# Evacuating filler banks with priority, and transposing the GLA keys ahead of the values, in a hybrid decoder layer

## The chip, the cores and the metric

The kernel runs on one core of a Trainium2 chip. Times are device microseconds of one execution, from which a median over several runs is taken. The profile is of one execution. In it PE is TensorE's matmul queue, PEld its weight loads (they overlap with PE), DVE is VectorE, ACT is ScalarE, POOL is GpSimd, and SP issues most of the DMAs. L548 is line 548 of the kernel before.

## What is computed

One decoder layer on 512 tokens of width 1024, in float32:

- RMS norm of x, and one projection `w_in` that gives everything the two mixers need.
- A sparse attention (NSA) with 8 query heads in two key/value groups: compressed blocks, selected blocks (all 8 of 8 here), and a window of 256, each with its own softmax and a gate.
- A chunked gated linear attention (GLA) with 4 heads of key width 64 and value width 128, in chunks of 64: a state per chunk, decayed and added up from chunk to chunk, and an output from the chunk itself and from the state before it, then a norm and a gate.
- The two branches are projected, gated by a sigmoid (the merge) and summed, projected by `w_out` and added to x.
- A cross attention to 256 memory tokens, and a gated feed-forward layer of width 2816 with a convolution of width 3; each behind an RMS norm and added to x. A final RMS norm.

```
h = rms_norm(x, ln_mix_g)
q_a, kv_a, gate_a, q_b, k_b, v_b, r_b, alpha_b, merge = split(h @ w_in)
mix = sigmoid(merge_1) * (nsa(...) @ w_branch_nsa) + sigmoid(merge_2) * (gla(...) @ w_branch_gla)
x = x + mix @ w_out
x = x + memory_cross_attention(rms_norm(x), mem_n, ...)
x = x + conv_ffn(rms_norm(x), ...)
return rms_norm(x, ln_final_g)
```

## The kernel before

**Products.** Activations lie transposed, width on the partitions and the 512 tokens along the free axis. Each float32 operand is split in a high half (rounded to fp32r) and a low half (the rest), and each product is three matmuls: high by high, high by low, low by high (`mm3`, L159 to L162). `split` (L164 to L166) makes the halves: ACT copies into the high half (L165), DVE subtracts to get the low one (L166). `scaled_split` (L201 to L203) does it with a factor.

**Weights.** They come as 141 blocks of 128 x 1024 in the order of use. `take` (L153) hands out a block and makes `convert` (L130) prepare two blocks further: SP loads it (L126), ACT makes the high half (L140), and an engine out of the list `lo_engine`, by the block's number, makes the low half (L141). For the last eight blocks this is done in halves of 512 columns (L148 and L149). The list holds DVE alone at first; after the first four blocks it is DVE and GpSimd in turn, until the products that compress keys and values are done (L471), and DVE alone from then on.

**Banks.** PSUM has eight banks in four tags: `acc` 2, `sc` 3, `pt` 2, `o` 1. A tile of a tag waits until one of the tag's banks has been read for the last time. SBUF tiles come in tags too: `t` has 6 tiles of 512 columns, `s` 16, and `g` 43.

**Order.** Instructions are written in program order, and a scheduler orders them on each engine ahead of time, by its own estimate of when each is ready, with program order as the priority. Each engine then works through its queue in that order. What a block of code issued under high priority, its instructions go ahead of others that are ready at the same time.

**Fillers.** The attention stage (`nsa_scores`, `nsa_values`) is full of softmax work for DVE and ACT. Between its steps `fill` (L506) issues closures out of a list, each a dense product of 24 matmuls (`dense8`) into an `acc` bank, which is then evacuated: `gla_r` (four; its bank is read by DVE at L548, then ACT and GpSimd go on), `gla_q` (two, L523) and `gla_k` (two, L533). In the GLA stage the fillers are eight `nsa_part`: for each even one two merge products come first (`merge`, bank read by DVE at L717, then a tanh on ACT at L718), and each has a branch product (`branch`) whose bank is read at L741.

**GLA stage.** In program order: what is left of the fillers, the value projection (`dense_tok` into four banks, then `scaled_split` of each), and then for each of two pairs of heads (m): `gla_qk` splits queries and keys (L796 to L801), `gla_keys` transposes the decayed keys by four matmuls into a bank of tag `pt` (L750) and splits them into two `t` tiles, `gla_att` makes the scores within the chunks (L809) and masks them (L813), `gla_states` makes the increments (L764) into three banks of tag `sc` and one of `pt`, chains them on DVE (L774, L776) and splits the states, and `gla_out` (L834 to L844) and `gla_norm` (L243, L227, L228, L855, L856) finish a head. One `fill` stands between most of these steps:

```
    qk = {(0, a): gla_qk(0, a) for a in range(2)}
    ks = gla_keys(0)
    a0 = gla_att(*qk[0, 0])
    st = gla_states(0, *ks)
    fill(GLA_FILL[0])
    ...
    gla_norm(*o)
    o = gla_out(0, 1, st[1], *a1)
    ks = gla_keys(1)
    fill(GLA_FILL[3])
```

**The end.** The second half of the down projection makes the first 384 tokens of each of eight output tiles (`head_mm`, L160 to L162). `head_out` adds the residual (L1128) and calls `add_square`: ACT squares (L214), and GpSimd adds to the running sum (L224). After the first four tiles two tiny activations (L1137, L1138) bring in the table with the square root ahead of its use. The other 128 tokens follow, and among their matmuls the norm of the first 384 (`norm_head`, `scale_head`).

Of the kernel before, what the change touches and what calls it, by code (L numbers as in the profile page):

```python
# [16 lines left out]
P = 128  # L17
# [41 lines left out]
def layer_kernel(ctx: ExitStack, tc: tile.TileContext, xT, memT, W, small, const, gfin, out, out_t, order):  # L59
# [319 lines left out]

    V2 = [None] * 4  # L380
    pb = [bank(t) for t in ("sc", "sc", "pt", "o")]
    for b0, nk in ((0, 3), (3, 3), (6, 2)):
        w = take(("BB", b0, nk))
        for j in range(nk):
            k = b0 + j
            c = slice(j * BW, (j + 1) * BW)
            for t in range(4):
                ts = slice(t * P, (t + 1) * P)
                o = pb[t][:, :BW]
                nc.tensor.matmul(o, xg[k][0][:, ts], w[0][:, c], start=k == 0, stop=False)  # L390
                nc.tensor.matmul(o, xg[k][0][:, ts], w[1][:, c], start=False, stop=False)
                nc.tensor.matmul(o, xg[k][1][:, ts], w[0][:, c], start=False, stop=k == KT - 1)
    xk = cmp_inputs(pkc, S("pos_k"))
# [77 lines left out]
    lo_engine[:] = [nc.vector]  # L471
# [42 lines left out]
    def gla_q(m):  # L514
        def go():
# [7 lines left out]
            nc.vector.scalar_tensor_tensor(q, ps, 0.125, rstd, op0=ALU.mult, op1=ALU.mult)  # L523
# [4 lines left out]
    def gla_k(m):  # L528
        def go():
# [3 lines left out]
            nc.vector.tensor_mul(kf, ps, rstd)  # L533
# [10 lines left out]
    def gla_r(hd):  # L544
        def go():
            ps = dense8(("A", "w_in", C_RB + hd * P), xg)
            rf, th = t_(), t_()
            nc.vector.tensor_mul(rf, ps, rstd)  # L548
# [156 lines left out]
    fill(99)  # L705
    pb = [bank(t) for t in ("acc", "acc", "sc", "sc")]
# [7 lines left out]
    def merge(col, m, tile_):  # L714
        ps = dense8(("A", "w_in", col + m * P), xg)
        th = tile_()
        nc.vector.tensor_mul(th, ps, rstd)  # L717
        nc.scalar.activation(th, th, AF.Tanh, scale=0.5)  # L718
        return th
# [15 lines left out]
    def nsa_part(n):  # L735
        def go():
# [4 lines left out]
            nc.vector.scalar_tensor_tensor(pm[n], pm[n], 1.0, ps, op0=ALU.add, op1=ALU.mult)  # L741
# [4 lines left out]

    def gla_keys(m):
        pk = bank("pt")
        for t in range(4):
            nc.tensor.transpose(pk[:, t * P:(t + 1) * P], ksd[m][:, t * P:(t + 1) * P], C("ident"))  # L750
        kh, kl = t_(F32R), t_(F32R)
        split(kh, kl, pk)
        return kh, kl
# [108 lines left out]
    ks = gla_keys(0)  # L862
# [6 lines left out]
    o = gla_out(0, 0, st[0], *a0)  # L869
    fill(GLA_FILL[2])  # L870
    gla_norm(*o)
    o = gla_out(0, 1, st[1], *a1)
    ks = gla_keys(1)
# [253 lines left out]
    def head_out(ps, n):  # L1127
        nc.vector.tensor_add(x2[n][:, head], ps, x2[n][:, head])  # L1128
        add_square(sqs, x2[n][:, head], CUT)
# [7 lines left out]
    nc.scalar.activation(warm, x2[0][:, 0:1], AF.Square)  # L1137
    nc.scalar.activation(warm, warm, AF.Sqrt)  # L1138
    for n in range(4, 8):
# [3 lines left out]
        head_out(ps, n)  # L1143
    gt = sb([P, 1024], F32, "raw", 3)
# [171 lines left out]
```

## Time and profile before

| | us |
|---|---|
| median of 3 runs | 865.82 (863.78 to 866.4) |
| the profiled execution | 864.57 |
| its span, first to last instruction | 862.7 |
| PE busy | 847.2 |
| DVE busy | 565.8 |
| ACT busy | 425.0 |
| POOL busy | 176.6 |

The granted clock of TensorE was 0.998 of full speed over the span. Busy times count an engine's own instructions; matmuls are pipelined, and their ends are modelled, so a matmul's row is longer than the distance to the next one. An idle time in square brackets stands before the instruction, with what ended it.

### The profile page before, as it was taken

To read this page: it belongs to the slowest core of one execution; us is meant where nothing else is said; L and a number is where in the kernel's file an instruction comes from. 1 tells how busy PE (TensorE), PEld (TensorE's weight loads), DVE (VectorE), ACT (ScalarE), POOL (GpSimd) and SP (SyncE) were. 2 spreads that over 40 slices of the span, in tenths; PEclk is the share of its full clock that TensorE was granted. 3 is DMA by queue.
4 is the path that set the end of the run, shared out by engine and by line. 5 is a ranking of instruction groups with operands and counts; after the bars stand their busy time and mean duration, and the time that the engine had idled before them with its cause. 6 is when DMAs were issued, how large, how long until landed. Compare 5 with 4: busy or idle time off the path is not lost.

```text
span 862.7 us, 11076 instructions
## 1 busy us (share of the span) xinstructions
PE 847.2 (98%) x4172; PEld 706.4 (82%) x4172; DVE 565.8 (66%) x923; ACT 425.0 (49%) x742; POOL 176.6 (20%) x157
## 2 busy tenths in 40 slices
PE   9999999999999999999999999999999999999997
PEld 6988788777877888898888888888888888888996
DVE  7576898989979677454587759665533465565324
ACT  8466878787444455344455545433311333334311
POOL 2373354412000023203200412111000111112121
PEclk9999999999999999999999999999999999999999
DMA  8332210102221242254331132222222222222302
GB/s 292 115 131 98 74 50 25 49 25 74 74 91 57 74 147 98 97 178 147 123 115 49 65 110 96 98 98 97 98 98 98 97 98 98 97 98 98 123 25 98
DMA packets 26406, 83.58 MB, mean 97 GB/s; under 512 B 3056, under 2 KB 5104, under 8 KB 26352
## 3 DMA queue, kind: packets, MB, share of 16 engines
q1 hardware_dynamic: 26064, 82.58, 27.5%
q8 instruction: 33, 0.54, 0.2%
q10 hardware_dynamic: 288, 0.28, 0.1%
q14 instruction: 21, 0.17, 0.1%
HBM read 80.76 MB, written 2.10 MB: 96 GB/s over the span
## 4 chain that ended last, share of the span: by engine, by line
PE 87%; DVE 5%; ACT 4%; issue 1%; POOL 1%; DMA 0%; DVEq 0%; ACTq 0%; POOLq 0%
PE up_ps_sc L162 4%; PE up_ps_sc L161 4%; PE up_ps_sc L160 4%; PE fill_ps_acc L160 3%; PE fill_ps_acc L161 3%; PE fill_ps_acc L162 3%; PE up_ps_pt L162 3%; PE up_ps_pt L161 3%; PE up_ps_pt L160 3%; PE up_ps_acc L162 3%; PE up_ps_acc L161 3%; PE up_ps_acc L160 3%; PE nsa_ps_o L663 2%; PE nsa_ps_pt L669 2%; PE down_ps_sc L162 2%; PE down_ps_sc L161 2%
## 5 line engine op out<-in xcount | busy, mean ns | idle before, releaser
L1086 POOL TENSOR_TENSOR up_s<-up_s,up_s 128x512 f32<-128x512 f32 x22 | 35.8, 1630 | 259.1 <-ACT up_wh L140 207.0
L141 DVE TENSOR_TENSOR up_wl<-up_raw,up_wh 128x1024 fp32r<-128x1024 f32 x40 | 63.0, 1575 | 15.4 <-ACT up_wh L140 15.3
L140 ACT ACTIVATE up_wh<-up_raw 128x1024 fp32r<-128x1024 f32 x40 | 42.5, 1061 | 60.9 <-PE up_ps_sc L161 31.9
L160 PE MATMUL up_ps_sc<-xo_g,up_wh 128*128 128x512 f32 x124 | 48.3, 390 | 0.0
L162 PE MATMUL up_ps_sc<-xo_g,up_wl 128*128 128x512 f32 x124 | 48.3, 389 | 0.0
L161 PE MATMUL up_ps_sc<-xo_g,up_wh 128*128 128x512 f32 x124 | 48.3, 389 | 0.0
L160 PE MATMUL up_ps_pt<-xo_g,up_wh 128*128 128x512 f32 x104 | 40.5, 389 | 0.0
L162 PE MATMUL up_ps_pt<-xo_g,up_wl 128*128 128x512 f32 x104 | 40.5, 389 | 0.0
L161 PE MATMUL up_ps_pt<-xo_g,up_wh 128*128 128x512 f32 x104 | 40.5, 389 | 0.0
L160 PE MATMUL fill_ps_acc<-in_g,fill_wh 128*128 128x512 f32 x96 | 38.4, 400 | 0.8 <-DVE fill_t L548 0.8
L161 PE MATMUL fill_ps_acc<-in_g,fill_wh 128*128 128x512 f32 x96 | 38.1, 397 | 0.0
L162 PE MATMUL fill_ps_acc<-in_g,fill_wl 128*128 128x512 f32 x96 | 37.9, 395 | 0.0
L631 ACT ACTIVATE nsa_s<-nsa_s,nsa_nm 128x128 f32<-128x128 f32 (+3 forms) x64 | 34.2, 538 | 6.5 <-DVE nsa_nm L622 6.5
L160 PE MATMUL up_ps_acc<-xo_g,up_wh 128*128 128x512 f32 x88 | 34.3, 389 | 0.0
L162 PE MATMUL up_ps_acc<-xo_g,up_wl 128*128 128x512 f32 x88 | 34.3, 389 | 0.0
L161 PE MATMUL up_ps_acc<-xo_g,up_wh 128*128 128x512 f32 x88 | 34.2, 389 | 0.0
L1082 ACT ACTIVATE up_s<-up_s 128x512 f32<-128x512 f32 x22 | 13.8, 632 | 40.4 <-DVE up_s L1080 40.4
L140 ACT ACTIVATE down_wh<-down_raw 128x1024 fp32r<-128x1024 f32 x9 | 9.5, 1061 | 39.4 <-PE down_ps_sc L161 17.5
L165 ACT ACTIVATE nsa_pth<-nsa_ps_pt 128x512 fp32r<-128x512 f32 x38 | 21.9, 593 | 11.0 <-PE nsa_ps_pt L669 10.7
L161 PEld LDWEIGHTS up_ps_sc<-xo_g,up_wh 128*128 128x128 f32 x124 | 23.3, 188 | 4.9
L160 PEld LDWEIGHTS up_ps_sc<-xo_g,up_wh 128*128 128x128 f32 x124 | 23.3, 188 | 4.8
L162 PEld LDWEIGHTS up_ps_sc<-xo_g,up_wl 128*128 128x128 f32 x124 | 23.3, 188 | 4.8
(975 smaller groups left out, 2687.6 us busy)
## 6 DMA issues: line engine op xcount, KB each, us to landing
up_raw<-in_w SPq DMA_DIRECT2D x44, 512.0 KB, 3.2
fill_raw<-in_w SPq DMA_DIRECT2D x20, 512.0 KB, 3.2
down_raw<-in_w SPq DMA_DIRECT2D x18, 512.0 KB, 3.2
proj_raw<-in_w SPq DMA_DIRECT2D x14, 512.0 KB, 3.8
mix_raw<-in_w SPq DMA_DIRECT2D x12, 512.0 KB, 3.2
mkv_raw<-in_w SPq DMA_DIRECT2D x8, 512.0 KB, 3.3
wout_raw<-in_w SPq DMA_DIRECT2D x8, 512.0 KB, 3.4
in_s<-in_xT SPq DMA_DIRECT2D x8, 256.0 KB, 5.4
```

Of the source, the lines that this page charges most:

```text
L140: nc.scalar.activation(wh[:, c], r[:, c], AF.Copy)
L141: lo.tensor_tensor(wl[:, c], r[:, c], wh[:, c].bitcast(F32), op=ALU.subtract)
L160: nc.tensor.matmul(ps, w[0], x[0], start=first, stop=False)
L161: nc.tensor.matmul(ps, w[0], x[1], start=False, stop=False)
L162: nc.tensor.matmul(ps, w[1], x[0], start=False, stop=last)
L165: nc.scalar.activation(h, src, AF.Copy)
L631: nc.scalar.activation(s[:, :w], s[:, :w], AF.Exp, scale=sl, bias=nm[:, c:c + 1], accum_out=sums[:, c:c + 1])
L663: nc.tensor.matmul(po, v, x, start=j == 0 and x is parts[0], stop=j == last and x is parts[-1])
L669: nc.tensor.transpose(pt[:, g * P:(g + 1) * P], srcs[g], C("ident"))
L1082: nc.scalar.activation(cv, cv, AF.Gelu_apprx_tanh)
L1086: nc.gpsimd.tensor_tensor(gm, gm, cv, op=ALU.mult)
```

## The change

- A helper `evacuate` issues one operation at high priority. Five operations that read a filler's bank go through it: in `gla_q`, `gla_k`, `gla_r`, `merge` (also used in the mix stage) and `nsa_part`.
- `gla_keys` is defined earlier, and the keys of the first pair are transposed and split before the value projection. Those of the second pair come right after the first head's output, ahead of one more filler and of the second head's output. Their halves lie in `g` tiles instead of `t` tiles.
- `lo_engine` becomes DVE alone earlier: right after the blocks of the values, gates and alphas.
- In `head_out` the sums of squares are added on DVE instead of GpSimd.
- The two tiny activations for the square root's table come after the sixth tile instead of after the fourth.

```
+    def evacuate(op, *args, **kw):
+        with tc.high_priority():
+            op(*args, **kw)
...
+    lo_engine[:] = [nc.vector]
     xk = cmp_inputs(pkc, S("pos_k"))
...
     cmp_hidden("cmp_w1_v", xv, hid[0:62, P:2 * P], 1)
-    lo_engine[:] = [nc.vector]
...
-            nc.vector.scalar_tensor_tensor(q, ps, 0.125, rstd, op0=ALU.mult, op1=ALU.mult)
+            evacuate(nc.vector.scalar_tensor_tensor, q, ps, 0.125, rstd, op0=ALU.mult, op1=ALU.mult)
...
-            nc.vector.tensor_mul(kf, ps, rstd)
+            evacuate(nc.vector.tensor_mul, kf, ps, rstd)
...
-            nc.vector.tensor_mul(rf, ps, rstd)
+            evacuate(nc.vector.tensor_mul, rf, ps, rstd)
...
     stage[0] = "gla"
     fill(99)
+
+    def gla_keys(m):
+        pk = bank("pt")
+        for t in range(4):
+            nc.tensor.transpose(pk[:, t * P:(t + 1) * P], ksd[m][:, t * P:(t + 1) * P], C("ident"))
+        kh, kl = g_(F32R), g_(F32R)
+        split(kh, kl, pk)
+        return kh, kl
+
+    ks = gla_keys(0)
     pb = [bank(t) for t in ("acc", "acc", "sc", "sc")]
     dense_tok("w_in", C_VB, xg, pb)
...
-        nc.vector.tensor_mul(th, ps, rstd)
+        evacuate(nc.vector.tensor_mul, th, ps, rstd)
...
-            nc.vector.scalar_tensor_tensor(pm[n], pm[n], 1.0, ps, op0=ALU.add, op1=ALU.mult)
+            evacuate(nc.vector.scalar_tensor_tensor, pm[n], pm[n], 1.0, ps, op0=ALU.add, op1=ALU.mult)
...
-    def gla_keys(m):
-        pk = bank("pt")
-        for t in range(4):
-            nc.tensor.transpose(pk[:, t * P:(t + 1) * P], ksd[m][:, t * P:(t + 1) * P], C("ident"))
-        kh, kl = t_(F32R), t_(F32R)
-        split(kh, kl, pk)
-        return kh, kl
...
     qk = {(0, a): gla_qk(0, a) for a in range(2)}
-    ks = gla_keys(0)
     a0 = gla_att(*qk[0, 0])
...
     o = gla_out(0, 0, st[0], *a0)
+    ks = gla_keys(1)
     fill(GLA_FILL[2])
     gla_norm(*o)
     o = gla_out(0, 1, st[1], *a1)
-    ks = gla_keys(1)
     fill(GLA_FILL[3])
...
-        add_square(sqs, x2[n][:, head], CUT)
+        add_square(sqs, x2[n][:, head], CUT, eng=nc.vector)
...
     for n in range(4):
         head_out(banks[n], n)
-    nc.scalar.activation(warm, x2[0][:, 0:1], AF.Square)
-    nc.scalar.activation(warm, warm, AF.Sqrt)
     for n in range(4, 8):
...
         head_out(ps, n)
+        if n == 5:
+            nc.scalar.activation(warm, x2[n][:, 0:1], AF.Square)
+            nc.scalar.activation(warm, warm, AF.Sqrt)
```

## Rows read from the trace of the kernel before

**Rows 1.** The page's first part: busy time, share of the span and instruction count of each engine.

```profile
PE 847.2 (98%) x4172; PEld 706.4 (82%) x4172; DVE 565.8 (66%) x923; ACT 425.0 (49%) x742; POOL 176.6 (20%) x157
```

**Rows 2.** The view of waits, for the matmul queue alone: the waiting group, what released it, the total in us, how often, the longest.

```profile
PE fill_ps_acc L160 <- DVE fill_g L717: 1.5, 1, 1.5
...
PE gla_ps_sc L764 <- ACT gla_t L165: 1.2, 2, 0.8
PE nsa_ps_o L663 <- DVE nsa_ptl L166: 1.1, 2, 0.6
PE down_ps_sc L162 <- DVE down_g L149: 0.8, 2, 0.5
PE fill_ps_acc L160 <- DVE fill_t L548: 0.8, 1, 0.8
PE proj_ps_acc L162 <- POOL proj_wl L141: 0.5, 1, 0.5
PE nsa_ps_pt L669 <- DVE nsa_s L639: 0.4, 2, 0.2
PE gla_ps_sc L764 <- DVE gla_t L813: 0.3, 1, 0.3
PE gla_ps_sc L764 <- DVE gla_s L203: 0.2, 1, 0.2
```

**Rows 3.** The view of stretches: from and to in us, length, then the busy time (and instruction count) of PE, of its weight loads, of DVE, ACT and POOL, the granted clock, the DMA share and GB/s.

```profile
42.00:52.00 10.00, 9.48 (x64) 7.94 (x63) 7.57 (x20) 8.22 (x13) 5.23 (x7) 1.00 0.29 102
...
60.00:75.00 15.00, 15.00 (x108) 12.59 (x107) 9.04 (x15) 8.60 (x13) 7.89 (x6) 1.00 0.58 199
...
100.00:140.00 40.00, 38.48 (x201) 31.52 (x200) 35.84 (x117) 31.35 (x82) 16.20 (x18) 1.00 0.15 51
...
210.00:217.00 7.00, 6.14 (x43) 4.83 (x42) 6.22 (x13) 4.52 (x9) 0.00 (x0) 1.00 0.00 0
250.00:275.00 25.00, 22.66 (x124) 18.31 (x124) 24.26 (x39) 12.21 (x20) 1.05 (x2) 1.00 0.11 38
...
312.00:810.00 498.00, 497.88 (x2301) 416.53 (x2300) 295.91 (x352) 201.91 (x287) 78.98 (x50) 1.00 0.31 107
```

**Rows 4.** The timeline of DVE around 118 us, in the sparse attention: start, length, engine, line, operation, output and inputs, shapes, count, and the idle time before it with its releaser.

```profile
118.15 0.85 DVE L688 TENSOR_TENSOR nsa_t<-nsa_ps_o,nsa_t 64x256 f32<-64x256 f32 x2 [1.33 <-ACT nsa_t L683]
119.03 0.69 DVE L548 TENSOR_TENSOR fill_t<-fill_ps_acc,proj_rstd 128x512 f32<-128x512 f32 x1
```

**Rows 5.** The same view around 271 us, in the GLA stage. PE first, then DVE.

```profile
269.91 0.39 PE L161 MATMUL fill_ps_acc<-in_g,fill_wh 128*128 128x512 f32 x1
270.14 0.39 PE L162 MATMUL fill_ps_acc<-in_g,fill_wl 128*128 128x512 f32 x1
...
265.72 3.00 DVE L776 SCALAR_TENSOR_TENSOR gla_s<-gla_s,fill_dec,gla_ps_sc 64x128 f32<-64x128 f32 x8
...
272.64 0.69 DVE L717 TENSOR_TENSOR fill_g<-fill_ps_acc,proj_rstd 128x512 f32<-128x512 f32 x1
```

**Rows 6.** The same view around 256 us, where the second pair's key transposes are split. PE first, then ACT.

```profile
256.77 0.50 PE L764 MATMUL gla_ps_sc<-gla_s,gla_t 64*128 64x256 f32 x4 [0.84 <-ACT gla_t L165]
...
256.14 0.57 ACT L165 ACTIVATE gla_t<-gla_ps_pt 128x512 fp32r<-128x512 f32 x1
```

**Rows 7.** The same view from 211 to 215.5 us, at the end of the value projection. PE first, then DVE.

```profile
212.86 0.38 PE L764 MATMUL gla_ps_sc<-gla_s,gla_t 64*128 64x256 f32 x1 [0.38 <-ACT gla_t L165]
...
215.17 0.39 PE L764 MATMUL gla_ps_sc<-gla_s,gla_t 64*128 64x256 f32 x1 [0.29 <-DVE gla_t L813]
...
213.29 0.68 DVE L166 TENSOR_TENSOR gla_t<-gla_ps_pt,gla_t 128x512 fp32r<-128x512 f32 x1
...
214.39 0.72 DVE L813 COPY_PREDICATED gla_t<-in_cst,gla_ps_sc 128x512 f32<-128x512 uint32 x1
```

**Rows 8.** Line 141, the low halves of the weights: the timeline of POOL around 50 us, then, from the view of that line, its two groups in the projection stage on POOL and on DVE (shortest, median and longest in ns, first and last start).

```profile
48.88 2.40 POOL L141 TENSOR_TENSOR proj_wl<-proj_raw,proj_wh 128x1024 fp32r<-128x1024 f32 x1 [4.67 <-ACT proj_wh L140]
...
L141 POOL TENSOR_TENSOR proj_wl<-proj_raw,proj_wh x5: 2395/2411/2924, 38.1 to 67.1; 128x1024 fp32r<-128x1024 f32 x5
...
L141 DVE TENSOR_TENSOR proj_wl<-proj_raw,proj_wh x7: 1210/1227/2003, 24.0 to 69.7; 128x1024 fp32r<-128x1024 f32 x7
```

**Rows 9.** The timeline at the end of the down projection, around 817 us: ACT, then from the views of lines 149 and 224 the low halves on DVE and the sums of squares on POOL.

```profile
816.72 1.28 ACT L1138 ACT_TABLE_LOAD   x1
...
818.13 2.70 ACT L148 ACTIVATE down_g<-down_raw 128x512 fp32r<-128x512 f32 x5
...
834.69 0.53 ACT L214 ACTIVATE down_t<-wout_g 128x384 f32<-128x384 f32 x1 [5.19 <-DVE wout_g L1128]
...
L149 DVE TENSOR_TENSOR down_g<-down_raw,down_g x10: 676/684/1501, 802.0 to 822.6; 128x512 fp32r<-128x512 f32 x10
...
L224 POOL TENSOR_TENSOR down_g<-down_g,down_t x7: 1009/1016/1373, 816.0 to 841.1; 128x384 f32<-128x384 f32 x7
```

**Rows 10.** The timeline of ACT, PE and DVE: the last high half of the keys of the first head pair, the first matmul of the output of head 1, and the evacuation of the third and the fourth merge bank.

```profile
201.48 0.63 ACT L800 ACTIVATE gla_g<-fill_g 64x512 fp32r<-64x512 f32 x1
...
249.29 0.28 PE L834 MATMUL gla_ps_o<-gla_pth,gla_s 128*128 128x256 f32 x1
...
240.87 0.69 DVE L717 TENSOR_TENSOR fill_g<-fill_ps_acc,proj_rstd 128x512 f32<-128x512 f32 x1 [0.27 <-PE fill_ps_acc L162]
...
246.31 0.69 DVE L717 TENSOR_TENSOR fill_g<-fill_ps_acc,proj_rstd 128x512 f32<-128x512 f32 x1 [3.35 <-PE fill_ps_acc L162]
```

## The prediction

> **What bounds the kernel now.** First the page's busy times: PE is busy 847.2 of 862.7 us [rows 1], so only 15.5 us of PE's span are idle, and all that the change could win lies in PE's waits and not in its work: no matmul is added or taken away. A busy row hides a little more. The reader sees in the timeline that a 512-column matmul lasts 0.39 us but that the next one starts 0.23 us after it [rows 5]; a wait therefore costs PE its idle time and about 0.16 us more (0.39 less 0.23), and I add that to each below. Then the waits of the matmul queue alone [rows 2]: they are few, and nearly all are for DVE or ACT, in four places. Then the stretches [rows 3]: from 312 to 810 us PE is busy 497.88 of 498.00 us, so nothing can be won there, while in the attention and GLA stages DVE is the full engine (35.84 of 40 us from 100 to 140, 24.26 of 25 us from 250 to 275). There PE waits because DVE does something else first.
>
> **Profile and median.** The profiled execution took 864.57 us for a span of 862.7; the median of the runs, 865.82, stands 1.25 us above it. I make the sum against 864.57 and add 1.25 at the end. What a measurement here can tell from no change is about 0.3%, 2.6 us: 863.2 to 868.4.
>
> **Part by part.**
> Evacuation of the gla_r banks (L548): a filler's matmul waited 0.8 us [rows 2], with the overlap 0.96. DVE stood idle for 1.33 us for ACT with L688 at the head of its queue, ran it for 0.85, and only then L548, 0.69 us long [rows 4]; the bank had been full before. With priority L548 goes into the hole. Ends 0.3 (0.96 less the 0.69 if that now delays the softmax) and 0.96; I take 0.9, since the hole is longer than the instruction.
>
> Evacuation of the merge banks (L717): the longest wait of all, 1.5 us, with the overlap 1.66 [rows 2]. DVE ran the states' chain L776 from 265.72 on, then the splits, and L717 only at 272.64 [rows 5], though the bank is the older of two that PE filled before 270.4. With priority it goes some 7 us earlier, in the chain. The chain ends 0.69 later for it. Ends 0.3 and 1.66; I take 1.5, because what the chain feeds is covered by the next filler's 24 matmuls of 0.23 us.
>
> The other evacuations: seven more banks in the attention stage, where DVE is 90% busy. If each delays the softmax work by its 0.69 us on the path, 7 x 0.69 = 4.8 lost; if they come into holes and also free PE's four waits for nsa_ptl and nsa_s (1.1 + 0.4 us, with the overlap 2.1 [rows 2]), 2.1 won. I take a loss of 0.7, one of seven, since DVE has holes like the one at 118 us and the fillers are spread. The eight merges of the mix stage and the L741 groups I cost at nothing: no wait of PE is for L741, and PE has 0.12 us of idle time in all after 312 us [rows 2, 3].
>
> Keys before the values: the four transposes of each pair stay, PE's work is the same, but they no longer stand just ahead of the matmuls that need them. Second pair: PE waited 0.84 us for ACT's L165, which came at 256.14 behind other ACT work [rows 6], with the overlap 1.0. Issued a filler (over 5 us) earlier that wait goes; next in line is the release of a bank of tag sc, so ends 0.3 and 1.0, taken 0.9. First pair: three waits of 0.38, 0.2 and 0.3 us [rows 2, 7], with the overlap 1.36. The first was for the split of the keys and goes; the second is for the values' own split and stays; the third is for L813, which had DVE's 0.68 us of key split ahead of it [rows 7] and comes that much earlier at most. Ends 0.1 and 1.36; I take 0.7. Against it the key split moves into the attention stage's full DVE: 0 to 0.7, taken 0.3. The two keys move from the six t tiles to the 43 g tiles, priced as a rival below.
>
> Low halves to DVE: GpSimd did five, of 2.41 us [rows 8]; four of them (the blocks taken from the first key block on) go to DVE at 1.23 us. PE's wait for the one begun at 48.88 was 0.5 us, with the overlap 0.66 [rows 2, 8]. The DVE row of this size would end 1.2 us earlier, but behind the splits already queued; ends 0 and 0.66, taken 0.6. DVE gets 4 x 1.23 = 4.9 us more between 48 and 75 us. It has 2.43 free of 10 us in 42 to 52 and 5.96 of 15 in 60 to 75 [rows 3], which covers it; without that cover it would cost 4.9 less the 0.66. GpSimd gives up 9.6 us and its casts come sooner; nobody is seen to wait for those. In this place the Trainium skill speaks against the edit: "Perfetto Trace Analysis", Optimizing Scalar/DVE Operations, says that work should go the other way, from a saturated DVE to ScalarE or even GpSimd. By that rule the projection would get slower by part of the 4.9; the stretch shows DVE 60% busy and not saturated, so I go by the row.
>
> End of the down projection: PE waited twice for L149, 0.8 us together, with the overlap 1.1 [rows 2]. The table load L1138 held ACT for 1.28 us at 816.72, and the high halves L148 started only behind it at 818.13 [rows 9]; the low halves on DVE then ran beside GpSimd's sums, and went from 0.684 to up to 1.5 us [rows 9]. With the load two blocks later ACT is free 1.4 us earlier. The load then sits before the square at 834.69, where ACT had 5.19 us idle [rows 9]. DVE takes the sums, an estimated 0.53 us each (0.684 x 384/512) instead of 1.016 on GpSimd, three of them, 1.6 us, ahead of the low halves; DVE was idle there for ACT. Ends 0.5 and 1.1, taken 1.1. The last sum comes 0.5 us earlier, but PE does not wait for it [rows 2]: nothing. No DMA moves and no block's order changes, so SP's queue is as it was.
>
> Sum: 0.9 + 1.5 + 0.9 + 0.7 + 0.6 + 1.1 = 5.7 won, 0.7 + 0.3 = 1.0 lost, 4.7 net: 864.57 - 4.7 = 859.9, and with 1.25 **861.1 us**. All upper ends: 6.7 + 2.1 = 8.8 won, 857.0. All lower ends: 1.5 won, 0.7 + 4.8 = 5.5 lost, 869.8.
>
> **Rivals.**
> *Priority changes no order.* The queue of DVE is written out ahead of time; if the bank counts as full too late there, L717 and L548 stay where they are. Left: 0.9 + 0.7 + 0.6 + 1.1 - 0.3 = 3.0, so 862.8. For it: at 118 us DVE's queue had L688 ahead of a bank that was full. Against: at 271 us the bank was full for several us. Chance 0.14.
>
> *The waits move.* DVE is full, so what is put ahead delays what PE wants next: the 1.5 of L717 comes back as a wait for the states, the 0.9 of the keys as one for L813, and two more of the seven evacuations hit the path (1.4). 4.7 - 3.8 = 0.9, so 864.9. For it: 24.26 of 25 us, and DVE's 1.33 us idle at 118 us with work behind [rows 3, 4], which shows that its queue goes strictly in order; the Trainium skill says the same ("PSUM — Partial Sum Buffer", Engine vs sequencer instructions). Against: in most of these places PE has a filler's matmuls to go on with. Chance 0.22.
>
> *The g tiles run out, slower.* By my count from the code up to 43 of the 43 are live around the first pair's outputs once two keys lie there; at the end of attention the last tile of the first pair's keys already came only at 201.48 [rows 10]. It decides where a 44th is wanted. Then the third merge bank (evacuated at 240.87) keeps its contents until head 1's output has been read, from 249.29 on; PE, which filled the fourth by 246.31, would stand from there to 249.3 + 0.69, that is 3.7 us [rows 10]. The same again at the end of attention, and the 0.7 there not won: 7.4 + 0.7 - 4.7 = 3.4 slower, 869.2. Against: 43 just fits. Chance 0.11.
>
> **How the numbers follow.** Forecast 0.53, the others 0.14, 0.22, 0.11. Faster: 0.53 and half of the first rival (862.8 is close to 863.2), 0.60. Within 0.3%: 0.22 + 0.07 = 0.29. Slower: 0.11. The range goes from the sum of the upper ends, 857, to 867, which takes in the first two rivals and most of the unknown delays and leaves out the third.
>
> **What would show it.** Right: no PE wait for L717 and L548 and L717 ahead of the states' chain on DVE; no wait for ACT's key split; one L141 on GpSimd in the projection; the table load after 824 us and no wait for L149; some 5 us less idle PE. Wrong: new waits of PE for nsa_ptl, nsa_s or the states of over 2 us, or evacuations that sit on DVE idle for PE; then the gains were only moved.

## The result: 874.1 us against 865.1, slower

Four executions of the changed kernel took 873.69 to 876.26 us, median 874.14; the kernel before, beside it, 863.78 to 866.40, median 865.07. The ratio is 1.0108 with an interval of 1.0092 to 1.0125: slower by over 0.3%, where 861.1 us and faster was forecast.

The granted clock is needed to read what follows. TensorE runs at one of two levels, 2.4 and 1.2 GHz, and in some executions it falls to the lower one for some microseconds while there is still work, which lowers the mean granted clock that is recorded for the run. Of 148 executions of the kernel before that were taken beside the experiments, 79 show a mean of 0.998 or more and a median of 864.35 us, 41 show 0.996 and 865.96, 25 show 0.992 and 869.12; the other three show 0.997 and 864.67, the time of those without a fall. So I give for each kernel its median and also its level without a fall, the median of its executions at 0.998 or more. (The profiled execution of before has one stretch at 1.2 GHz too, from 859.05 us on; its last matmul starts at 856.18, so that it costs nothing.) All four executions of the changed kernel show 0.989 to 0.991; there is none without a fall.

### The profile page after: what moved, and what is told of

Its sections match the earlier page's. It is cut to its first block, busy times and chain, and to the rows that moved or that the text cites. A ratio compares the mean times of both kernels' runs of the same rounds, so it can differ in the third digit from the quotient of the medians.

```text
span 872.3 us, 11078 instructions
## 1 busy us (share of the span) xinstructions
PE 854.3 (98%) x4172; PEld 710.5 (81%) x4172; DVE 580.6 (67%) x934; ACT 424.2 (49%) x742; POOL 161.1 (18%) x146
## 4 chain that ended last, share of the span: by engine, by line
PE 84%; DVE 8%; ACT 5%; POOL 2%; issue 1%; DVEq 0%; POOLq 0%; ACTq 0%
PE up_ps_sc L161 4%; PE up_ps_sc L162 4%; PE up_ps_sc L160 4%; PE fill_ps_acc L161 3%; PE fill_ps_acc L162 3%; PE fill_ps_acc L160 3%; PE up_ps_pt L161 3%; PE up_ps_pt L162 3%; PE up_ps_pt L160 3%; PE up_ps_acc L161 2%; PE up_ps_acc L162 2%; PE up_ps_acc L160 2%; PE down_ps_sc L162 2%; PE down_ps_sc L161 2%; PE down_ps_sc L160 2%; ACT nsa_s L636 1%
## 5 line engine op out<-in xcount | busy, mean ns | idle before, releaser
L166 DVE TENSOR_TENSOR nsa_ptl<-nsa_ps_pt,nsa_pth 128x512 fp32r<-128x512 f32 x38 | 25.5, 683 | 6.4 <-ACT nsa_pth L165 6.3
L674 PE MATMUL nsa_ps_pt<-in_cst,nsa_s 128*128 128x128 f32 x152 | 25.6, 285 | 3.0 <-DVE nsa_s L644 2.8
L674 PEld LDWEIGHTS nsa_ps_pt<-in_cst,nsa_s 128*128 128x128 f32 x152 | 18.9, 144 | 11.2 <-DVE nsa_s L644 6.3
```

The lines of the kernel that those rows point to most:

```text
L166: nc.vector.tensor_sub(l, src, h.bitcast(F32))
L674: nc.tensor.transpose(pt[:, g * P:(g + 1) * P], srcs[g], C("ident"))
```

## The profile after

Part 1 of the page answers to [rows 1]:

```profile
PE 854.3 (98%) x4172; PEld 710.5 (81%) x4172; DVE 580.6 (67%) x934; ACT 424.2 (49%) x742; POOL 161.1 (18%) x146
```

PE has the same 4172 matmuls and is busy 7.1 us longer: they did not only wait longer, some ran slower. The waits of the matmul queue, which answer to [rows 2] (total us, times, longest):

```profile
PE nsa_ps_pt L674 <- DVE nsa_s L644: 2.8, 6, 1.1
PE nsa_ps_o L668 <- ACT nsa_pth L165: 1.9, 1, 1.9
PE nsa_ps_o L668 <- DVE nsa_ptl L166: 1.7, 3, 0.6
...
PE nsa_ps_o L668 <- DVE proj_pc L166: 1.1, 1, 1.1
PE gla_ps_sc L771 <- DVE gla_s L203: 0.8, 1, 0.8
PE proj_ps_acc L162 <- DVE proj_wl L141: 0.8, 1, 0.8
PE gla_ps_sc L771 <- DVE gla_t L851: 0.6, 1, 0.6
...
PE down_ps_sc L162 <- DVE down_g L149: 0.2, 1, 0.2
```

The waits that the forecast went for are gone: none for L548 and L717 any more, none for ACT's key split, 0.2 instead of 0.8 for L149. In their place stand waits of the attention stage, for nsa_s (2.8, was 0.4), for ACT's nsa_pth (1.9, was none), for nsa_ptl (1.7, was 1.1) and for proj_pc (1.1, was none). The stretches, which answer to [rows 3] (busy us and number of PE, PEld, DVE, ACT, POOL; granted clock; DMA):

```profile
100.00:140.00 40.00, 37.74 (x195) 29.98 (x194) 38.41 (x113) 31.10 (x81) 15.98 (x17) 1.00 0.18 64
140.00:147.00 7.00, 5.09 (x27) 3.52 (x26) 4.77 (x8) 4.74 (x11) 6.26 (x7) 1.00 0.00 0
147.00:154.00 7.00, 6.46 (x20) 4.73 (x20) 4.93 (x12) 4.30 (x19) 0.78 (x1) 0.51 0.00 0
...
217.00:226.00 9.00, 8.18 (x43) 6.47 (x42) 8.74 (x19) 6.75 (x14) 0.00 (x0) 0.97 0.00 0
226.00:233.00 7.00, 7.00 (x22) 5.20 (x21) 5.54 (x16) 1.35 (x3) 0.00 (x0) 0.55 0.00 0
250.00:275.00 25.00, 24.32 (x124) 19.93 (x123) 19.19 (x23) 10.71 (x15) 1.05 (x2) 1.00 0.25 85
```

and two of them in the kernel before:

```profile
140.00:147.00 7.00, 6.70 (x40) 5.38 (x39) 4.62 (x11) 6.42 (x22) 5.84 (x6) 1.00 0.00 1
147.00:154.00 7.00, 7.00 (x40) 5.60 (x39) 6.60 (x19) 6.16 (x14) 1.54 (x3) 1.00 0.08 20
```

The reader is to look at the granted clock, the column after POOL's. It falls to 0.51 from 147 to 154 us and to 0.55 from 226 to 233; the trace's records of the clock put the falls at 146.97 to 153.80 and 225.48 to 232.31 us, 6.83 us each. Both come just after PE had idled: 1.91 of 7 us from 140 to 147, 0.82 of 9 from 217 to 226. From 147 to 154 us PE is busy for 6.46 of 7 us and does 20 matmuls, where it did 40 in 7.00.

Where the time went can be added up. For each matmul I took the time to the next one's start, less the usual time for its shape (the 40th percentile over both traces), which counts waits and the lower clock alike:

| stretch, us | before | after | after less before |
|---|---|---|---|
| 0 to 100 | 3.4 | 3.5 | +0.1 |
| 100 to 140 | 3.2 | 4.8 | +1.6 |
| 140 to 160 | 2.1 | 6.6 | +4.5 |
| 160 to 210 | 5.3 | 7.3 | +2.0 |
| 210 to 250 | 1.5 | 5.8 | +4.3 |
| 250 to 300 | 3.5 | 2.1 | -1.4 |

That is 11.1 us lost by 300 us, 8.1 of them in attention; the last filler matmul before the memory stage starts at 309.6 instead of 298.5. The end gives 1.2 back: the last matmul starts at 866.03, not 856.18, 9.85 later.

The stall ahead of the first fall can be read in three rows. ACT, from 141 to 147 us:

```profile
141.59 0.71 ACT L646 ACTIVATE nsa_s<-nsa_s,nsa_cf 128x512 f32<-128x512 f32 x1
144.52 0.63 ACT L541 ACTIVATE fill_t<-fill_t 128x512 f32<-128x512 f32 x1 [2.22 <-POOL fill_t L539]
145.06 0.49 ACT L165 ACTIVATE nsa_g<-nsa_t 128x128 fp32r<-128x128 f32 x2
145.46 0.61 ACT L543 ACTIVATE fill_g<-fill_g 128x512 f32<-128x512 f32 x1
146.09 1.08 ACT L165 ACTIVATE nsa_pth<-nsa_ps_pt 128x512 fp32r<-128x512 f32 x2
```

GpSimd, before that:

```profile
140.31 2.63 POOL L650 TENSOR_SCALAR nsa_s<-nsa_s,nsa_cf 128x384 f32<-128x384 f32 x2
142.92 0.57 POOL L651 TENSOR_TENSOR proj_cm<-proj_cm,nsa_cf 128x124 f32<-128x124 f32 x1
143.45 1.04 POOL L539 TENSOR_TENSOR fill_t<-fill_g 128x512 f32<-128x512 f32 x1
```

and PE:

```profile
146.75 0.62 PE L668 MATMUL nsa_ps_o<-nsa_pth,proj_g 128*128 128x512 f32 x1 [1.89 <-ACT nsa_pth L165]
```

ACT stands idle for 2.22 us with L541, gla_k's exponential, at the head of its queue. That waits for GpSimd's subtraction L539, which GpSimd has in its queue behind the two softmax scalings L650 (2.63 us) and L651, and runs without a pause after them. Behind L541 on ACT stand the splits nsa_g and the copy nsa_pth that PE needs; both of ACT's nsa_pth come at 146.09, PE has idled for 1.89 us, and 0.2 us after it goes on its clock falls. In the kernel before L534 (the same subtraction) ran ahead of the scalings (L645 there), and ACT took its result (L536, the exponential) without a wait:

```profile
136.48 1.04 POOL L534 TENSOR_TENSOR fill_t<-fill_g 128x512 f32<-128x512 f32 x1
...
140.32 2.85 POOL L645 TENSOR_SCALAR nsa_s<-nsa_s,nsa_cf 128x384 f32<-128x384 f32 x2 [0.20 <-issue]
...
139.60 0.62 ACT L536 ACTIVATE fill_t<-fill_t 128x512 f32<-128x512 f32 x1
```

## Experiments

The theory after the traces: **the early attention banks rearrange the fixed queues so that ACT stands behind GpSimd; the stall, and the falls of the clock that come with stalls, are the loss.** Rivals: the key tiles (my rival of before), VectorE filled up by the low halves, and a clock that falls by chance whatever the order.

**The four parts alone**, each added to the kernel before.

```diff
+    def evacuate(op, *args, **kw):      # p1: the five evacuations
+        with tc.high_priority():
+            op(*args, **kw)
...
-    ks = gla_keys(1)                    # p2: both pairs' keys early, in g tiles
...
+    lo_engine[:] = [nc.vector]          # p3: ahead of cmp_inputs
...
-        add_square(sqs, x2[n][:, head], CUT)                  # p4: and warm after n == 5
+        add_square(sqs, x2[n][:, head], CUT, eng=nc.vector)
```

> The kernel before with only the five priority evacuations. Theory 1 (the evacuations reorder the attention stage: ACT stands behind GpSimd's subtraction for gla_k, PE idles over 1.5 us once, and its granted clock then falls from 2.4 to 1.2 GHz for 6.83 us): the stall near 144 us and one fall of the clock there are in this run, while the end of GLA is not hurt; about 8 us lost in attention, 1.5 to 2 won at the merges: 870 to 872 us, ratio near 1.007. Theory 2 (the key tiles taken from the g tiles are what costs): no more than 1 us from before, 864 to 866, no fall of the clock before 800 us. Theory 3 (low halves on VectorE fill it up): the same as theory 2 here.

> The kernel before with only the key transposes moved and their tiles taken from the g tiles. Theory 1: attention as before; the second fall of the clock (225 us) belongs to this part if the early keys bunch the states' small matmuls behind the values: then 864 + 2 to 4, 867 to 869; if it needs the evacuations too, no fall and 863 to 864. Theory 2 (tiles run out): 868 or more, with PE or the split waiting for a g tile and no fall of the clock needed. Theory 3: 864 to 865.

> The kernel before with only the low halves of four more blocks on VectorE. Theory 1 and theory 2: 864.5 to 865.5, no change; PE's wait for proj_wl near 50 us stays at 0.8 since VectorE's queue is as late as GpSimd was. Theory 3 (these halves delay VectorE's queue into the attention stage): 868 or more, with waits for nsa_s and nsa_ptl.

> The kernel before with only the end: the sums of squares of the head on VectorE and the table load two blocks later. All theories: faster by the 1.1 us that the two waits for L149 cost, 864.0 against 865.1, and the trace ends its last matmul 1.1 us earlier; nothing before 810 us moves.

| kernel | median us | ratio to before, interval | without a fall |
|---|---|---|---|
| p1, evacuations | 870.36 | 1.0048 (1.0027 to 1.0068) | 868.71 (1 of 8) |
| p2, keys | 867.41 | 1.0018 (1.0003 to 1.0034) | 867.01 |
| p3, low halves | 865.34 | 0.9999 (0.9978 to 1.0019) | 864.41 |
| p4, end | 864.35 | 0.9986 (0.9969 to 1.0003) | 863.23 |

Against 864.35 without a fall the end wins 1.1 us, as expected; the low halves change nothing, and PE's wait near 50 us is now 0.8 for VectorE where it was 0.5 for GpSimd. The evacuations carry the attention loss: p1's trace has the same stall and a fall from 146.54 to 153.37 us. The keys alone cost 2.7 us without a fall. That is within the 867 to 869 of theory 1, but not for its reason, a fall near 225 us: no g tile is waited for either, and the fall in p2's trace (259.88 to 263.29 us) comes on top. Neither p1's nor p2's trace has the fall at 225 us.

p4 also shows what a fall is worth. Its queues are those of before up to 810 us, and the profiled execution (867.99 us) has these stretches:

```profile
210.00:215.00 5.00, 4.24 (x31) 3.21 (x29) 4.22 (x10) 3.80 (x7) 0.00 (x0) 1.00 0.00 0
215.00:222.00 7.00, 6.89 (x20) 5.51 (x21) 6.55 (x19) 1.81 (x4) 0.00 (x0) 0.51 0.22 76
270.00:276.00 6.00, 4.96 (x28) 4.14 (x27) 5.65 (x14) 3.62 (x6) 0.00 (x0) 1.00 0.00 0
276.00:280.00 4.00, 3.55 (x9) 2.78 (x10) 3.90 (x5) 2.25 (x4) 0.00 (x0) 0.57 0.36 116
```

The same order of instructions ran with 6.8 us at the lower clock after the small waits of [rows 7], and 3.4 us after the one of [rows 5], and took 4.8 us longer than p4's 863.23: 0.47 us for each us at 1.2 GHz, about the half that PE then loses. By that rate the 13.65 us of the changed kernel cost 6.4 us, and its level without a fall is near 867.7 (an estimate, since it has no such execution): 3.4 us of waits, net of what the other parts win, and the rest is the clock.

**Without the attention priority, and three neighbours.** q1 is the changed kernel with the priority taken back at gla_q, gla_k and gla_r; q2 keeps all priorities and moves one instruction; q3 and q4 add parts to the kernel before.

```diff
-            evacuate(nc.vector.tensor_mul, rf, ps, rstd)          # q1, and so for q and kf
+            nc.vector.tensor_mul(rf, ps, rstd)
...
-            nc.gpsimd.tensor_tensor(e3.rearrange(...), ..., cv, op=ALU.subtract)   # q2
+            nc.vector.tensor_tensor(e3.rearrange(...), ..., cv, op=ALU.subtract)
...
+        evacuate(nc.vector.tensor_mul, th, ps, rstd)              # q3: merge and nsa_part, and the end
...
+    ks = gla_keys(0)                                              # q4: first pair's keys alone
```

> The changed kernel with its priority taken back at the attention fillers alone (gla_q, gla_k, gla_r); merges, keys, low halves and end as changed. Theory 1 (those evacuations cost 4 to 5 us of waits in attention and bring the fall of TensorE's clock near 147 us, 3.4 us): no fall there, the 1.9 us wait for ACT's nsa_pth gone, 866 us (874.1 less 8). Theory 2 (the keys and their tiles are what costs): 873 or more, since the keys are still there. Theory 3 (the clock falls by chance, whatever the order): still two falls, 872 or more.

> The changed kernel with gla_k's subtraction on VectorE in place of GpSimd, so that ACT's exponential no longer stands behind GpSimd's queue. Theory 1a (the 2.1 us stall at 144 us is ACT waiting for GpSimd's L539, and the fall of the clock follows from it): stall and first fall go, 868.5 to 869.5. Theory 1b (the early evacuations cost by VectorE's instructions stretched beside GpSimd's, here and elsewhere): the stall is replaced by others, VectorE's nsa_g splits stay near 0.63 us, the fall may stay; 871 or more.

> The kernel before with the priority at the merges and nsa_part alone, and the changed end; keys, low halves and attention as before. Theory 1: the 1.5 us wait for L717 goes with the fall of the clock that can follow it at 276 us, and the two waits for L149: 864.3 less 1.6 less 1.1, 861.6 where the clock does not fall, some 862 as median, ratio 0.996 to 0.997. Theory 2: the same. A theory that any priority costs: 865 or more.

> The kernel before with only the first pair's keys ahead of the values (in g tiles). In the run with both pairs the first pair's place had 0.8 us for the states and then a new 1.5 us wait for a merge's bank (L717's line) at 227 us, the second pair a new 1.0 us wait behind ACT's split at 257 us. If the first pair's move is what makes the 227 us wait: 865.5 to 866 where the clock does not fall (864.3 with 0.6 of waits gone and 1.7 new). If it needs the second pair: 863.8. Tiles running out would show as a wait of a split for a g tile and 3 us or more.

| kernel | median us | ratio to before, interval | without a fall |
|---|---|---|---|
| q1, changed without attention priority | 861.94 | 0.9960 (0.9944 to 0.9975) | 861.94 (10 of 11) |
| q2, subtraction on VectorE | 865.32 | 0.9987 (0.9971 to 1.0002) | 863.85 |
| q3, merges and end | 863.08 | 0.9967 (0.9952 to 0.9982) | 861.45 (5 of 12) |
| q4, first pair's keys | 867.25 | 1.0020 (1.0006 to 1.0035) | 866.56 |

q1 settles which part it is: 12.2 us come back, 4 more than the 8 expected, and both falls go, that at 225 us too, though the keys are still there. q2 does better than either branch: its ACT idles 0.38 us for L541, PE 0.4 for nsa_pth, no trace of a fall is left there, and the first branch had 3 to 4 us more. q3 is 2.9 us below before without a fall: 1.1 for the end and 1.8 for the banks of the merges and of nsa_part. q4 went the way of its first branch: its PE waits

```profile
PE fill_ps_acc L160 <- DVE fill_g L726: 3.0, 2, 1.5
...
PE gla_ps_pt L243 <- ACT gla_sqh L165: 0.8, 1, 0.8
PE gla_ps_sc L765 <- DVE gla_t L814: 0.7, 1, 0.7
```

name the merges' line twice (3.0 us in all, was once 1.5), so early keys put VectorE's splits ahead of the merges' banks there. In q1 that line has priority, and the wait does not exist.

**Which of the attention banks.** r1 to r3 are the changed kernel with the priority at two or one of the three; r4 is q3 with the keys.

```diff
-            evacuate(nc.vector.tensor_mul, kf, ps, rstd)           # r1: gla_k off; r2: gla_k, gla_q off
+            nc.vector.tensor_mul(kf, ps, rstd)                     # r3: gla_r, gla_q off
```

> The changed kernel with the priority taken back at gla_k alone. On ACT's queue its exponential, which waits for GpSimd, then stands behind the nsa_g split but still ahead of nsa_pth. Theory A (the 2.1 us stall and the fall of the clock come from gla_k's own bank): 864 to 866. Theory B (the block comes of all the early banks together, gla_r and gla_q having moved the order before gla_k's turn): stall of 1 to 2 us still there, the fall in most executions, 870 to 873.

> The changed kernel with the priority kept at gla_r and the merges, taken back at gla_q and gla_k. ACT's exponential then stands ahead of the softmax scales, as before the change. Theory B: no stall at 144 us and no fall there; the wait of 0.8 for L548's bank gone as forecast; 861 to 862 against 861.9 with none of the attention banks, plus up to 1 us for VectorE's stretched instructions. Theory C (gla_r is what costs, by GpSimd's work falling beside VectorE's): 865 or more.

> The changed kernel with the priority kept at gla_k and the merges, taken back at gla_q and gla_r. Theory A: 868 or more, with the stall of ACT behind GpSimd's L539. Theory B: 861.5 to 862.5, as with none of the attention banks, since the order on ACT around the exponential is that of before.

> The kernel before with the merges' priority, the keys of both pairs moved and the changed end; low halves on GpSimd as before, no priority in attention. Against the same without the keys (861.5 where the clock does not fall, 863.1 as median) the keys are the one difference. Forecast of the prediction's step (0.9 + 0.7 - 0.3 won): 860.2 without falls. Theory D (alone the keys cost 2.3 us by the merges' banks, with the priority that is mended, and what they win is that the clock falls less often near 215 us): 861.7 to 862.0 as median, hardly any execution with a fall.

| kernel | median us | ratio to before, interval | without a fall |
|---|---|---|---|
| r1, gla_r and gla_q early | 871.24 | 1.0070 (1.0050 to 1.0089) | none of 6 |
| r2, gla_r early | 865.98 | 1.0010 (0.9996 to 1.0023) | 865.59 |
| r3, gla_k early | 861.99 | 0.9967 (0.9952 to 0.9981) | 861.75 |
| r4, merges, keys, end | 861.99 | 0.9966 (0.9953 to 0.9980) | 861.75 |

By r1 and r3 theory B holds on the banks: gla_k's own is harmless, they are not when taken together. r1 has ACT idle 1.51 us behind L539 and PE 1.3 us behind nsa_pth; the fall that theory B put there is not in its trace, whose falls start at 221.83 and 266.20 us. r2 has no such stall ahead of nsa_pth and still costs 3.7 us more than q1, as theory C had it, so there is a second way; it begins at 120 to 130 us. VectorE's softmax scaling L644 and GpSimd beside it in q1 (start and duration in us, count at the end):

```profile
121.83 1.64 POOL L556 TENSOR_SCALAR fill_t<-fill_t 128x512 f32<-128x512 f32 x1 [6.22 <-ACT fill_t L554]
...
122.25 1.43 DVE L644 TENSOR_SCALAR nsa_s<-nsa_s,nsa_cf 128x384 f32<-128x384 f32 x3
...
123.45 2.57 POOL L650 TENSOR_SCALAR nsa_s<-nsa_s,nsa_cf 128x384 f32<-128x384 f32 x2
...
126.34 1.28 POOL L557 TENSOR_TENSOR fill_g<-fill_t,fill_t 128x512 f32<-128x512 f32 x1
```

and the same in r2:

```profile
123.40 1.50 POOL L556 TENSOR_SCALAR fill_t<-fill_t 128x512 f32<-128x512 f32 x1 [1.16 <-ACT fill_t L554]
...
124.64 2.49 DVE L644 TENSOR_SCALAR nsa_s<-nsa_s,nsa_cf 128x384 f32<-128x384 f32 x3
...
124.98 1.28 POOL L557 TENSOR_TENSOR fill_g<-fill_t,fill_t 128x512 f32<-128x512 f32 x1
...
126.24 2.58 POOL L650 TENSOR_SCALAR nsa_s<-nsa_s,nsa_cf 128x384 f32<-128x384 f32 x2
```

With gla_r's bank early the scalings start 2.39 us later (124.64, not 122.25) and take 2.49 us instead of 1.43, with GpSimd's product L557 now beside them; PE then waits 0.89 us for nsa_s, and over 120 to 140 us it loses 2.6 us where q1 loses 0.3. r4 shows that the keys win nothing where the merges have priority (861.75 against q3's 861.45), as theory D had it. Its median is 1.1 us lower than q3's because 8 of its 12 executions show no fall, and 5 of q3's; whether the keys make falls rarer cannot be told from so few.

**Moving the work off GpSimd, with controls.** s1 is r2 and s2 is q1, both with gla_r's two GpSimd instructions as one on VectorE; s3 is the changed kernel with that and q2's move; s4 is q1 with q2's move.

```diff
-            nc.gpsimd.tensor_scalar(th, th, 1.0, None, op0=ALU.add)
-            nc.gpsimd.tensor_tensor(s, th, rf, op=ALU.mult)
+            nc.vector.scalar_tensor_tensor(s, th, 1.0, rf, op0=ALU.add, op1=ALU.mult)
```

> Priority at gla_r and the merges only (that run: 866.0), with gla_r's two GpSimd instructions, (th + 1) and times rf, as one instruction on VectorE. Theory P (GpSimd beside VectorE stretches the softmax scaling, 2.49 us for three instead of 1.43): the scaling is back near 1.4 us, the loss of 2 us from 120 to 140 mostly gone, 862.5 to 864. Theory O (the order on VectorE costs, with or without GpSimd): 865.5 to 867, since VectorE has four instructions of 0.7 us more.

> The control: the same move of gla_r's two instructions to VectorE with no attention bank given priority (that run without the move: 861.9). Both theories: 861.5 to 863.5, within 1.5 us of 861.9. If it gains over 1 us, then s1 says less on the priority.

> The changed kernel, all its priorities kept, with gla_r's two instructions and gla_k's subtraction on VectorE (with the subtraction alone: 865.3). Theory P: 862 to 864, no fall of the clock before 200 us, and the evacuations' own gain (0.8 us at L548's bank) seen. Theory O: 865 or more.

> The control of the run with gla_k's subtraction on VectorE: the same move with no attention bank given priority (without the move: 861.9). If that run's 8.8 us came of ACT's block that goes: 861.5 to 862.5 here. If the move wins by itself: 860 or less.

| kernel | median us | ratio to before, interval | without a fall |
|---|---|---|---|
| s1 | 867.72 | 1.0029 (1.0016 to 1.0042) | 866.99 |
| s2, control of s1 | 864.17 | 0.9980 (0.9966 to 0.9993) | 862.77 |
| s3 | 863.93 | 0.9987 (0.9974 to 1.0000) | 863.92 (12 of 12) |
| s4, control of q2 | 867.94 | 1.0032 (1.0019 to 1.0045) | 866.36 (1 of 12) |

s2 and s3 came as theory P or both theories had them (s3 with no fall in any execution). Two missed. s1 was to be 862.5 to 864 if GpSimd's neighbourhood were the second way; it is slower than r2, and without a fall it lies 4.2 us above its control s2, as r2 lies 3.7 above q1. So gla_r's early bank costs as much with its GpSimd work gone. But s1 does not take the stretching away: its three scalings take 2.06 us, now beside GpSimd's scalings, and those of its control 1.69. What goes is most of PE's wait for them (0.2 us, where r2 has 0.89), and the loss moves: s1 loses 0.8 us more than s2 from 120 to 140 us, where r2 loses 2.3 more than q1, and 1.5 more from 160 to 210. The stretching by gla_r's GpSimd work is real and is no more than a part of it; that the order on the queues is the rest (theory O) is what is left, and is not shown. s4 was to be 862 and is 6.0 us above q1 by the medians (4.4 in its one execution without a fall): the same move that saved 8.8 us by the medians in q2 costs 6.0 here. A move rearranges all queues anew, and what decides is the order that results. s4's trace says so. Its ACT:

```profile
141.50 0.71 ACT L646 ACTIVATE nsa_s<-nsa_s,nsa_cf 128x512 f32<-128x512 f32 x1
146.27 0.31 ACT L631 ACTIVATE proj_cm<-proj_cm 128x124 f32<-128x124 f32 x1 [4.06 <-POOL proj_cm L630]
...
146.99 1.09 ACT L165 ACTIVATE nsa_pth<-nsa_ps_pt 128x512 fp32r<-128x512 f32 x2
```

and its GpSimd:

```profile
141.68 2.63 POOL L650 TENSOR_SCALAR nsa_s<-nsa_s,nsa_cf 128x384 f32<-128x384 f32 x2
...
144.63 1.25 POOL L544 TENSOR_TENSOR fill_g<-fill_t,fill_g 128x512 f32<-128x512 f32 x1
145.85 0.39 POOL L630 TENSOR_TENSOR proj_cm<-proj_cm,nsa_nm 128x124 f32<-128x124 f32 x1
```

Now L631, the compressed branch's exponential, stands ahead of nsa_pth on ACT, and GpSimd has L630, which it needs, behind the same two scalings: ACT is idle for 4.06 us and PE for 2.8.

**The copies with priority too.** u1 is the changed kernel, u2 is q1, with the split in nsa_values issued with priority, so that nsa_pth should come ahead.

```diff
-                split(h, l, pt)
+                with tc.high_priority():
+                    split(h, l, pt)
```

> The changed kernel, all its priorities kept, with the split of the transposed weights in nsa_values (ACT's copy nsa_pth and VectorE's nsa_ptl) issued with priority as well; no operation changes engine. On ACT's queue gla_k's exponential then stands ahead of the softmax scales again, as before the change. Theory order (ACT standing behind GpSimd ahead of nsa_pth makes the stall and the fall at 147 us): no stall over 1 us and no fall there, 863 to 866. Theory chance (any execution falls when so much is shifted): 870 or more.

> The version with no priority at the attention fillers (861.9) with the same priority at nsa_values' splits. PE's waits for nsa_ptl (1.2 us in all) may go: 860.5 to 861.5. If these splits take VectorE from the softmax: 862.5 to 864.

u1: 868.97 us, ratio 1.0028 (1.0013 to 1.0044), 867.59 without a fall. u2: 864.22, 0.9988 (0.9972 to 1.0003), 864.08 without a fall. u1 missed; u2 lies just above its second branch. u1 got gla_k's exponential out of the way, and the median is 5 us below the changed kernel's, but the stall is there again: ACT idles 2.08 us for GpSimd's L630, PE 2.2 for nsa_pth, and no clock falls at that place in the profiled execution. And the priority for nsa_values brings a new wait of 1.7 us for proj_pc at 100 us in both.

Read together, the traces agree on one thing. Between 138 and 149 us ACT idles 1.3 to 4.1 us for GpSimd in eight kernels (changed, p1, r1, r2, s1, s2, s4, u1); in each the instruction that it waits for (L539, or L630; the numbers shift by one or two between kernels) sits on GpSimd behind the two scalings L650, 2.6 to 3.1 us. In six of the eight PE then waits 1.1 to 2.8 us for nsa_pth; in r2 and s1 ACT's first two copies come before its idle time, and PE waits 0.4 and 0.9. A fall follows within the microsecond in two of the six, the changed kernel and p1. In the other kernels GpSimd has it ahead of them, or ACT takes its result later, and ACT waits for GpSimd 0.4 us at most. In q1 GpSimd runs

```profile
136.18 1.04 POOL L539 TENSOR_TENSOR fill_t<-fill_g 128x512 f32<-128x512 f32 x1
139.42 0.39 POOL L630 TENSOR_TENSOR proj_cm<-proj_cm,nsa_nm 128x124 f32<-128x124 f32 x1 [2.21 <-DVE nsa_nm L627]
140.02 2.85 POOL L650 TENSOR_SCALAR nsa_s<-nsa_s,nsa_cf 128x384 f32<-128x384 f32 x2 [0.20 <-issue]
```

and its ACT, which never waits for GpSimd there:

```profile
139.29 0.62 ACT L541 ACTIVATE fill_t<-fill_t 128x512 f32<-128x512 f32 x1
...
141.96 0.29 ACT L631 ACTIVATE proj_cm<-proj_cm 128x124 f32<-128x124 f32 x1
...
143.21 1.09 ACT L165 ACTIVATE nsa_pth<-nsa_ps_pt 128x512 fp32r<-128x512 f32 x2 [0.57 <-PE nsa_ps_pt L674]
```

## Why the prediction was wrong

**The failed step is "The other evacuations".** It took a loss of 0.7 us for seven attention banks, between 2.1 won and 4.8 lost; with the 0.9 of the L548 step the eight banks together were to win 0.2. Measured, with everything else of the change in place, the eight cost 12.2 us (874.14 against 861.94; 11.8 if each is taken against the kernel before beside it). Two assumptions failed in it. First, the bound of 4.8 priced what an early bank does on VectorE's queue alone, 0.69 us each. The banks' followers on ACT and GpSimd moved too, and the largest stall, 1.9 us, arose on ACT behind GpSimd, between two queues that I had not read. My own second rival rested on queues being strict; I applied it to VectorE and to GLA, and its place was attention. Second, I priced a wait as its idle time and 0.16 us for the overlap. In this kernel a wait can cost half of the 6.83 us after it as well: some 6.4 of the 12.2 us are falls of the clock, by the rate of p4. That the stall brings on the first fall is not shown beyond this: the changed kernel and p1 have both, q1 and q2 neither, and s4 and u1 the stall alone. No row that I read showed one with work to do, but the spread of the times did: 863.78 to 866.40 is two of the three levels above.

**The L548 evacuation** (0.9): the wait went, and the stretch from 100 to 120 us is 0.3 us better (2.82 to 2.49), the lower end; but gla_r, whose bank it is, alone costs 3.7 us further on. The hole on VectorE was there. What was not free is not found: what follows the bank came earlier as well, but without gla_r's GpSimd instructions (s1) the cost is the same.

**The L717 evacuation** (1.5): right, 1.8 won (q3's 2.9 less the end's 1.1), and PE loses 0.1 us from 270 to 280 where it lost 1.8.

**Keys ahead** (0.9 and 0.7 won, 0.3 lost): wrong. Alone they cost 2.7 us, through the merges' banks; with the merges mended, 0.3. What they were to save came back as waits for VectorE: r4 waits 0.7 us for gla_t L818 and 0.6 for L849 in the places of [rows 6, 7]. That is the second rival, much as it was worded. The 43 g tiles held; no trace shows a wait for one, so the third rival falls though its sign was right.

**Low halves** (0.6): the lower end, 0. VectorE ends no sooner at 50 us than GpSimd did, and the wait there is even 0.3 us longer. The rule that the prediction weighed against this edit (the Trainium skill, "Perfetto Trace Analysis", Optimizing Scalar/DVE Operations: taking work off a saturated DVE may make sense) was read as making the stage slower; the trace shows 1.9 us beyond the usual spacing from 42 to 75 us, where it was 2.0, so here the direction of the move did not matter.

**End** (1.1): right, 1.1, with one wait of 0.2 us left for L149 and the table load at 839.44 us in a gap of ACT of the changed kernel. Two figures of the prediction read wrong without touching its sum: 0.684 x 384/512 is 0.51, not 0.53, and the sums on VectorE took 0.56; and the 0.12 us of idle PE are those up to 810 us, not all after 312.

"Priority changes no order" falls at once: the orders changed, more than was wanted. The sum of the steps without attention was 4.5 us won; measured 2.7 by the medians (q1) and 2.4 without falls.

What stays open: why the clock falls after some stalls and not others (s4's 2.8 us had no fall in its profiled execution, the changed kernel's 1.9 us had one), what the second fall of the changed kernel needs (p1 and q1 have none near 225 us in their traces, but r1, s1 and s2 fall between 221 and 225 us, and p4, with the order of before, at 215), and which reordering it is, among those that gla_r's early bank brings, that costs its 3.7 us.

The version to keep is r4: the kernel before with priority at the merges' banks only, the early keys and the new end, 861.99 us, 0.34% below before (0.20 to 0.47%). q1, which has the low halves too, and r3 lie within 0.1 us of it; q3, without the keys, is 0.3 us below it where no execution falls and 1.1 above it by the medians.

## What to carry to other kernels

An early evacuation is not one instruction moved: everything that hangs on the bank moves on every queue, so read the queues of all engines around each place, and ask for each waiting instruction what stands behind it. Give priority where PE is seen to wait for that very bank and the followers are few (the merges), and leave it off where three engines are already interleaved closely. Where time has two or three levels for the same order of instructions, compare kernels at the same granted clock, and price a stall with the fall that may follow.

## What the runs showed that was not expected

TensorE's granted clock fell to 1.2 GHz in the middle of a kernel whose PE is 98% busy, for 3.41 or 6.83 us each time that a trace shows it, and in p4 each us of it cost 0.47 us. The eleven falls that the traces show with work to do lie in three places: at 146.5 to 147 us (changed, p1), at 215 to 225.5 (changed, p3, p4, r1, s1, s2) and at 260 to 276.6 (p2, p4, r1). In the 8 us before each PE had idled for 0.7 to 1.9 us. Which executions had one differed for one and the same kernel (66 of 148 of before, by time and mean clock). The Trainium skill ("TensorE: Matmul & The Clock Gate", What's actually happening) says that the clock follows how busy PE has been recently and that runs of one kernel differ in it. The traces agree on the second. On the first they agree only in part: each fall came after waits, but s4's PE idled 3.7 of the 8 us before 147.7 us and its clock did not fall, and r1's idled 0.7 us ahead of a fall. The longest single gap ahead of one was 1.9 us.

VectorE's short instructions lasted longer beside GpSimd's products: the fourteen 128x128 splits nsa_g between 100 and 210 us took 302 ns each in the mean in the kernel before and 634 in the changed one (the medians are alike, 283 and 288 ns over all sixteen), pairs up to 2.54 us at 145.38 us beside L545 and L544, where 0.48 is usual. The Trainium skill ("SBUF — State Buffer", Who interferes with whom) says that VectorE's instructions with two inputs in SBUF contend with a GpSimd instruction that reads SBUF; these rows agree. It says that VectorE's tensor_scalar can contend too, in its fast modes, and there the rows are mixed: L644 took 2.49 us beside the product L557 in r2, but 1.43 mostly beside the tensor_scalar L556 in q1, and L643, the same, 2.06 beside the tensor_scalar L649 in s1.
